# Fused two-block transformer: what fills TensorE beside a recurrent branch, and which engine squares the decays

## The chip, the cores and the metric

The kernel runs on one core of one Trainium2 chip. The metric is the device time of one execution in microseconds: 1811.38 us, the median of three runs (1807.41, 1811.38 and 1813.76). Lower is better. The core's engines are TensorE (PE, with its weight loads PEld), VectorE (DVE), ScalarE (ACT), GpSimd (POOL) and SyncE (SP), which issues most of the DMAs.

## The reference, cut to what matters

Two blocks run one behind the other on 512 tokens of width 1024 (plus 16 meta tokens in the first). The change lies in the second block, ahead of its experts. There one normalised input h is projected to q, k, v, to the input and the gate of a recurrent branch, and to two output gates:

```
q, k, v, lru_x, lru_g, gate_pre = split(h @ w_in)
o = diff_attention(rope(rms_norm(q)), rope(rms_norm(k)), v, lam)      # 8 heads, two 64-wide maps each
xr = depthwise_conv(lru_x)
for each direction:
    r, i = sigmoid(xr @ w_a + b_a), sigmoid(xr @ w_i + b_i)           # 8 diagonal blocks of 128
    log_a = -8 * r * softplus(-lam_param);  a = exp(log_a)
    h_dir = scan(a, sqrt(-expm1(2 * log_a)) * (i * xr))
y_lru = (h_fwd + h_bwd) * gelu(lru_g)
merged = g_attn * (norm(o) @ w_attn_o) + g_lru * (y_lru @ w_lru_o)
```

## The kernel before, in words

Everything is kept feature-major in float32. Each large matrix product is made of three matmuls on high and low halves (`mm3`, lines 151 to 153): the weights are loaded by SP in pieces of 1 MB into one of two raw buffers (line 68), ScalarE rounds 1024 columns to the high half (line 145) and VectorE subtracts for the low half (line 146). One such split feeds 24 matmuls of 512 columns, which is one filling step.

A build-time planner orders the instructions of each engine. It takes them by their place in the program and by when it reckons them ready, and may draw later ones forward where an earlier one is not ready. So the generators below give a place in the program, not a fixed time.

Stages that matter, in the order of the program (`block2`):

- **Recurrent branch.** Four groups of two 128-channel blocks. For each block, xr is split to rH and rL (lines 1023 and 1024), four gates are multiplied, and for each direction ScalarE makes two tanh (lines 1034 and 1035), the decay `a` by Exp (line 1036) and another tanh (line 1037); GpSimd squares the decay into `a2` (line 1039), and VectorE makes (a2 + 1) times that tanh (line 1040). Line 1041 forms the gated input on VectorE. At the group's end ScalarE takes the square roots (line 1047, with a load of its table), VectorE multiplies and scans in both directions (lines 1049 to 1051), and GpSimd adds the two scans into `hs`. Behind each group the program takes filling steps: 5, 5, 4 and 4.
- **The filling there** is the projection of q, k and v for the first four heads, then gelu tiles. `qkv2` takes k, q, v in turn, four steps each, and holds four PSUM banks through the four steps. k and q are emptied by ScalarE (a square), by VectorE (lines 1260 to 1262) and by GpSimd (line 1266), then scaled (line 1279 for k); v is emptied by four ScalarE copies (line 1253). A gelu tile takes one bank and one step; `ev_gelu2` empties it by five VectorE and three ScalarE instructions (lines 1001 to 1008), one of which multiplies by `hs`, and leaves lH and lL.
- **Attention 2, first half.** Heads 0 to 3, four steps a head, with more filling: the gelu tiles that are left, the eight tiles of the recurrent branch's output projection (each needs all eight lH and lL; ScalarE copies them out at line 1061), and q, k, v of heads 4 to 7. Nothing is taken at the first two steps, two items at each further one.
- **Attention 2, second half.** Heads 4 to 7, filled by the tiles of the two output gates.

PSUM has four banks for filling in the recurrent branch and the first half (`ps2`), two for scores, one for transposes, one for values. Most large tensors live in a pool of 30 pair buffers (`big`, two tiles of 528 columns each); a new tile waits until one of them is let go.

```python
gelu = self.fm_steps(wi["lru_g"], KD, 8, xH, xL, C0, ev_gelu2)
fill = chain(self.qkv2(0, wi, xH, xL, inv, epsx, qkv[0]), gelu)
...
nc.gpsimd.tensor_tensor(a2, a[:, dd], a[:, dd], op=ALU.mult)
...
for _ in range(5 if grp < 2 else 4):
    next(fill, None)
```

Of the kernel before, what the change touches and what calls it, by code (L numbers as in the profile page):

```python
# [11 lines left out]
F32 = mybir.dt.float32  # L12
# [4 lines left out]
AF = mybir.ActivationFunctionType  # L17
ALU = mybir.AluOpType
AX = mybir.AxisListType

P = 128
D = 1024
KD = D // P
SEQ = 512
# [110 lines left out]
class Builder:  # L135
# [779 lines left out]
    def block2(self, xH, xL, squares, out):  # L915
        nc, A, tc = self.nc, self.A, self.tc
        V, S, E = nc.vector, nc.scalar, nc.tensor
        with ExitStack() as ctx:
# [6 lines left out]
            wi = {k: Weights(self, A["w2_" + k], 1024, 2)  # L925
                  for k in ("q", "k", "v", "lru_x", "lru_g", "g_attn", "g_lru")}
            vx = sm.tile([P, 4], F32, name="vx")
            inv = sm.tile([P, 4], F32, name="inv2")
            inv_b = med.tile([P, SEQ], F32, name="inv_b2", bufs=1)
            epsx = sm.tile([P, 4], F32, name="epsx2")  # L930
# [3 lines left out]
            sp = sm.tile([P, 16], F32, name="sp")  # L934
# [15 lines left out]
            V.tensor_scalar(t, t, 0.0, 0.5, op0=ALU.max, op1=ALU.mult)  # L950
            V.tensor_tensor(sp, sp, t, op=ALU.add)
            spm = {}
            for f in (-8.0, 8.0):
                spm[f] = sm.tile([P, 16], F32, name=f"sp{int(f) + 16}")
                V.tensor_scalar(spm[f], sp, f, None, op0=ALU.mult)
            hb = {}
            for w in ("a", "i"):
# [51 lines left out]

            qkv = [{}, {}]  # L1010
            gelu = self.fm_steps(wi["lru_g"], KD, 8, xH, xL, C0, ev_gelu2)
            fill = chain(self.qkv2(0, wi, xH, xL, inv, epsx, qkv[0]), gelu)
            wl = Weights(self, A["w2_lru"], 1024, 1)
            for grp in range(4):
                wH, wL = [t.rearrange("p (n m c) -> p n m c", n=2, m=4) for t in wl.get(grp)]
                units = []
                for nn in range(2):
                    n = 2 * grp + nn
                    rH = med.tile([P, SEQ], F32R, name="rH", tag="hl")
                    rL = med.tile([P, SEQ], F32R, name="rL", tag="hl")  # L1020
                    ix = med.tile([P, 2, SEQ], F32, name="ix", tag="pr")
                    a, m2 = self.pair("la", F32, (P, 2, SEQ)), self.pair("lm", F32, (P, 2, SEQ))
                    S.copy(rH, xr[n])
                    V.tensor_tensor(rL, xr[n], rH.bitcast(F32), op=ALU.subtract)
                    for dd in range(2):
                        u = 8 * dd + n
                        if dd == 0:
                            pr, pi = [self.ps_sc.tile([P, SEQ], F32, name="sc") for _ in range(2)]
                        else:
                            pr = self.ps_tr.tile([P, SEQ], F32, name="tr")  # L1030
                            pi = self.ps_pv.tile([P, SEQ], F32, name="pv")
                        self.mm3(pr, wH[:, nn, 2 * dd], wL[:, nn, 2 * dd], rH, rL, True, True)
                        self.mm3(pi, wH[:, nn, 2 * dd + 1], wL[:, nn, 2 * dd + 1], rH, rL, True, True)
                        S.activation(m2[:, dd], pr, AF.Tanh, scale=0.5, bias=hb["a"][:, u:u + 1])
                        S.activation(ix[:, dd], pi, AF.Tanh, scale=0.5, bias=hb["i"][:, u:u + 1])
                        S.activation(a[:, dd], m2[:, dd], AF.Exp, scale=spm[-8.0][:, u:u + 1], bias=spm[-8.0][:, u:u + 1])
                        S.activation(m2[:, dd], m2[:, dd], AF.Tanh, scale=spm[8.0][:, u:u + 1], bias=spm[8.0][:, u:u + 1])
                        a2 = med.tile([P, SEQ], F32, name="a2", tag="pT", bufs=2)
                        nc.gpsimd.tensor_tensor(a2, a[:, dd], a[:, dd], op=ALU.mult)
                        V.scalar_tensor_tensor(m2[:, dd], a2, 1.0, m2[:, dd], op0=ALU.add, op1=ALU.mult)  # L1040
                    V.scalar_tensor_tensor(ix, ix, 1.0, xr[n][:, None, :].to_broadcast([P, 2, SEQ]),
                                           op0=ALU.add, op1=ALU.mult)
                    units.append((n, a, m2, ix))
                zero = sm.tile([P, 1], F32, name="zero", bufs=2)
                V.tensor_scalar(zero, units[-1][2][:, 1, :1], 0.0, None, op0=ALU.mult)
                for n, a, m2, ix in units:
                    S.activation(m2, m2, AF.Sqrt, scale=0.25, bias=zero)
                for n, a, m2, ix in units:
                    V.tensor_tensor(ix, ix, m2, op=ALU.mult)
                    V.tensor_tensor_scan(hs[n], a[:, 0], ix[:, 0], 0.0, op0=ALU.mult, op1=ALU.add)  # L1050
                    V.tensor_tensor_scan(m2[:, 1, ::-1], a[:, 1, ::-1], ix[:, 1, ::-1], 0.0, op0=ALU.mult, op1=ALU.add)
                    nc.gpsimd.tensor_tensor(hs[n], hs[n], m2[:, 1], op=ALU.add)
                for _ in range(5 if grp < 2 else 4):
                    next(fill, None)
# [14 lines left out]
            def ev_gattn(m, ps, c0, n):  # L1069
# [7 lines left out]
            o = {}  # L1077
            fill = chain(gelu,
                         self.fm_steps(Weights(self, A["w_lru_o_2"], 1024, 2), KD, 8, lH, lL, C0, ev_lru_o),
                         self.qkv2(1, wi, xH, xL, inv, epsx, qkv[1]))  # L1080
            for step, _ in enumerate(self.attention2(0, qkv[0], ld, gs, o)):
                for _ in range(2 if step >= 2 else 0):
                    next(fill, None)
            for _ in fill:
                pass
            fill = chain(self.fm_steps(wi["g_lru"], KD, 8, xH, xL, C0, ev_glru),
                         self.fm_steps(wi["g_attn"], KD, 8, xH, xL, C0, ev_gattn))
# [134 lines left out]
            V.tensor_tensor(Sn[:, :, 32:], Sn[:, :, 32:], g[:, None, :32].to_broadcast([P, 4, 32]), op=ALU.mult)  # L1222
            self.TC2[w], self.TS2[w] = C, Sn

    def qkv2(self, b, wi, xH, xL, inv, epsx, out):

        nc = self.nc
        V, S = nc.vector, nc.scalar
        sm, med = self.sm, self.med
        if b == 0:  # L1230
            self.rope2_tables()
        for w in ("k", "q", "v"):
            tl = []
            for j in range(0, 4, 2):
                t = self.pair(w + "t", F32, (P, 2, SEQ))
# [3 lines left out]
            for i in range(4):  # L1239
                wH, wL = [t.rearrange("p (k c) -> p k c", k=2) for t in wi[w].get(4 * b + i)]  # L1240
                for j in range(4):
                    ts = slice(j * P, (j + 1) * P)
                    for kk in range(2):
                        k = 2 * i + kk
# [5 lines left out]
            for j in range(4):  # L1250
                ps = pss[j]
                if w == "v":
# [12 lines left out]
                                op=ALU.mult)  # L1265
# [546 lines left out]
```

## Time and profile before

| what | value |
|---|---|
| median of three runs | 1811.38 us |
| the profiled execution's own time | 1810.2 us |
| its span, first to last instruction | 1808.2 us |
| mean granted TensorE clock | 0.984 |
| TensorE busy | 1740.5 us, 96% |
| VectorE busy | 1215.0 us, 67% |
| ScalarE busy | 925.2 us, 51% |
| GpSimd busy | 264.8 us, 15% |
| recurrent branch, groups 0 to 3 | from 936 us to about 1090 us |
| attention 2, first half | to about 1246 us |

Times in the profile are microseconds from the span's start. Busy shares of the whole span are means over stages that have different limits, so the stages are looked at one by one. In a row of the timeline the bracket at the end is the engine's idle time just before, and what ended it. The granted clock is a mean over a stretch: 1.00 is 2.4 GHz, and at 1.2 GHz it would be 0.50.

### The profile page before, as it was taken

The numbers are of one execution on the slowest core, as the hardware profiler recorded it, in microseconds if no ns is written. First come the engines' busy times: TensorE is split into PE (matmuls) and PEld (weight loads), VectorE is DVE, ScalarE is ACT, GpSimd is POOL, SyncE is SP. The second block draws the span as 40 slices with busy tenths as digits, with TensorE's granted clock in tenths as the row PEclk, the third lists the DMA queues.
The fourth block names the chain that finished last, engine by engine and source line by source line (L and its number), as shares of the span: only waits on it lengthen the run. The fifth ranks groups of instructions, "written<-read, shape, count | busy, mean of one in ns | idle before, by whom it ended". The sixth has DMA issues, their size and how long they took to land. (4 is left out here: it accounts for less than half of the span.)

```text
span 1808.2 us, 25732 instructions
## 1 busy us (share of the span) xinstructions
PE 1740.5 (96%) x9706; PEld 1466.3 (81%) x9706; DVE 1215.0 (67%) x2264; ACT 925.2 (51%) x1545; POOL 264.8 (15%) x249
## 2 busy tenths in 40 slices
PE   7999999999999999999999898999999997999997
PEld 7889899999976878888877676777787886888885
DVE  7475555456457555446599988586776528999996
ACT  5343244433344234433336666545665335888885
POOL 3102300001210320000203321020101031111111
PEclk9999999999999999999999999999999997999999
DMA  4122121224322122223522222222115588999993
GB/s 146 59 89 71 53 69 51 75 77 142 109 77 93 53 70 70 70 82 106 170 90 70 85 90 71 70 70 70 53 65 190 184 282 298 384 383 387 381 383 64
DMA packets 69089, 244.36 MB, mean 135 GB/s; under 512 B 10848, under 2 KB 20064, under 8 KB 57056
## 3 DMA queue, kind: packets, MB, share of 16 engines
q1 hardware_dynamic: 63200, 221.69, 34.3%
q0 software_dynamic: 4608, 16.78, 3.6%
q10 hardware_dynamic: 1152, 4.19, 0.7%
q8 instruction: 78, 1.28, 0.3%
q14 instruction: 51, 0.42, 0.1%
HBM read 225.20 MB, written 17.37 MB: 134 GB/s over the span
## 5 line engine op out<-in xcount | busy, mean ns | idle before, releaser
L145 ACT CAST wh<-raw 128x1024 fp32r<-128x1024 f32 (+2 forms) x206 | 212.0, 1030 | 415.9 <-PE mm L152 335.7
L146 DVE TENSOR_TENSOR wl<-raw,wh 128x1024 fp32r<-128x1024 f32 (+2 forms) x206 | 253.4, 1232 | 103.9 <-ACT wh L145 102.2
L151 PE MATMUL mm<-xH,wh 128*128 128x264 f32 (+1 forms) x912 | 292.3, 321 | 10.8 <-ACT xH L361 8.7
L152 PE MATMUL mm<-xL,wh 128*128 128x264 f32 (+1 forms) x912 | 291.4, 320 | 0.7 <-DVE xL L362 0.5
L153 PE MATMUL mm<-xH,wl 128*128 128x264 f32 (+1 forms) x912 | 290.7, 319 | 0.0
L146 DVE TENSOR_TENSOR wl<-we,wh 128x1024 fp32r<-128x1024 f32 x192 | 227.5, 1222 | 15.7 <-ACT wh L145 13.0
L145 ACT CAST wh<-we 128x1024 fp32r<-128x1024 f32 x192 | 198.4, 1049 | 42.2 <-PE mm L153 32.5
L151 PEld LDWEIGHTS mm<-xH,wh 128*128 128x128 f32 x912 | 174.7, 192 | 24.0 <-ACT xH L361 8.7
L152 PEld LDWEIGHTS mm<-xL,wh 128*128 128x128 f32 x912 | 174.4, 192 | 11.5 <-DVE xL L362 1.4
L153 PEld LDWEIGHTS mm<-xH,wl 128*128 128x128 f32 x912 | 174.6, 192 | 10.4
L151 PE MATMUL mm<-wh,eH 128*128 128x512 f32 x256 | 104.4, 408 | 0.0
L151 PE MATMUL mm<-x2H,wh 128*128 128x512 f32 x256 | 102.1, 399 | 0.0
L152 PE MATMUL mm<-x2L,wh 128*128 128x512 f32 x256 | 101.9, 398 | 0.0
L153 PE MATMUL mm<-x2H,wl 128*128 128x512 f32 x256 | 101.8, 398 | 0.0
L153 PE MATMUL mm<-wh,eL 128*128 128x512 f32 x256 | 101.3, 396 | 0.0
L152 PE MATMUL mm<-wl,eH 128*128 128x512 f32 x256 | 101.0, 394 | 0.0
L126 POOL TENSOR_TENSOR z<-z,sq 128x528 f32<-128x528 f32 (+1 forms) x26 | 43.2, 1664 | 330.3 <-ACT sq L365 256.7
L151 PE MATMUL mm<-wh,x2H 128*128 128x512 f32 x192 | 77.5, 404 | 4.8 <-DVE rt__9342 L1262 2.8
L152 PE MATMUL mm<-wl,x2H 128*128 128x512 f32 x192 | 76.5, 399 | 0.0
L153 PE MATMUL mm<-wh,x2L 128*128 128x512 f32 x192 | 76.5, 402 | 0.0
L789 ACT ACTIVATE pr<-sc,bi,r3q 128x264 f32<-128x264 f32 (+3 forms) x80 | 46.6, 589 | 55.0 <-DVE bi L787 54.3
L151 PE MATMUL mm<-mgH,wh 128*128 128x264 f32 (+1 forms) x192 | 61.7, 321 | 0.0
(621 smaller groups left out, 4052.0 us busy)
## 6 DMA issues: line engine op xcount, KB each, us to landing
we<-in_w_moe SPq DMA_DIRECT2D x184, 512.0 KB
raw<-in_w_out SPq DMA_DIRECT2D x12, 1024.0 KB
raw<-in_w_g_mla SPq DMA_DIRECT2D x8, 1024.0 KB
raw<-in_w_g_pool SPq DMA_DIRECT2D x8, 1024.0 KB
raw<-in_w_c_q SPq DMA_DIRECT2D x6, 1024.0 KB
raw<-in_w_q_b SPq DMA_DIRECT2D x6, 768.0 KB
raw<-in_w_z_mla SPq DMA_DIRECT2D x4, 1024.0 KB
raw<-in_w_u_pool SPq DMA_DIRECT2D x4, 1024.0 KB
```

Of the source, the lines that this page charges most:

```text
L126: self.kb.nc.gpsimd.tensor_tensor(self.sum[:, off:], self.sum[:, off:], sq[:, off:], op=ALU.add)
L145: nc.scalar.copy(H[:, :F], src)
L146: lo.tensor_tensor(L[:, :F], src, H[:, :F].bitcast(F32), op=ALU.subtract)
L151: mm(out, lH, rH, start=start, stop=False)
L152: mm(out, lH, rL, start=False, stop=False)
L153: mm(out, lL, rH, start=False, stop=stop)
L789: S.activation(pr[:, a:b, e], scs[q], AF.Exp, bias=bi[:, e:e + 1], scale=c, accum_out=su[:, e, q:q + 1])
```

## The change

Three edits, all in the second block. First, the filling of the recurrent branch has v of heads 4 to 7 put between q, k, v of heads 0 to 3 and the gelu tiles; 18 steps are taken there as before, so 12 of the first half, 4 of v and 2 gelu tiles. Second, attention 2's first half is then filled by six gelu tiles, the output projection and k, q of heads 4 to 7 (22 items as before), with one item taken at each of the first two steps, where none was. Third, `a2` is made by ScalarE as Exp with twice the factor, from the tanh ahead of the one that overwrites it, and no longer by GpSimd as a product; a third scaled column, spm[-16.0], serves it.

```diff
-            for f in (-8.0, 8.0):
-                spm[f] = sm.tile([P, 16], F32, name=f"sp{int(f) + 16}")
+            for f in (-16.0, -8.0, 8.0):
+                spm[f] = sm.tile([P, 16], F32, name=f"sp{int(f) + 16}_")
                 V.tensor_scalar(spm[f], sp, f, None, op0=ALU.mult)
...
-            fill = chain(self.qkv2(0, wi, xH, xL, inv, epsx, qkv[0]), gelu)
+            fill = chain(self.qkv2(0, wi, xH, xL, inv, epsx, qkv[0]), self.qkv2(1, wi, xH, xL, inv, epsx, qkv[1], "v"), gelu)
...
                         S.activation(a[:, dd], m2[:, dd], AF.Exp, scale=spm[-8.0][:, u:u + 1], bias=spm[-8.0][:, u:u + 1])
+                        a2 = med.tile([P, SEQ], F32, name="a2", tag="pT", bufs=2)
+                        S.activation(a2, m2[:, dd], AF.Exp, scale=spm[-16.0][:, u:u + 1], bias=spm[-16.0][:, u:u + 1])
                         S.activation(m2[:, dd], m2[:, dd], AF.Tanh, scale=spm[8.0][:, u:u + 1], bias=spm[8.0][:, u:u + 1])
-                        a2 = med.tile([P, SEQ], F32, name="a2", tag="pT", bufs=2)
-                        nc.gpsimd.tensor_tensor(a2, a[:, dd], a[:, dd], op=ALU.mult)
...
-                         self.qkv2(1, wi, xH, xL, inv, epsx, qkv[1]))
+                         self.qkv2(1, wi, xH, xL, inv, epsx, qkv[1], "kq"))
             for step, _ in enumerate(self.attention2(0, qkv[0], ld, gs, o)):
-                for _ in range(2 if step >= 2 else 0):
+                for _ in range(2 if step >= 2 else 1):
                     next(fill, None)
...
-    def qkv2(self, b, wi, xH, xL, inv, epsx, out):
+    def qkv2(self, b, wi, xH, xL, inv, epsx, out, names="kqv"):
...
-        for w in ("k", "q", "v"):
+        for w in names:
```

## Rows read from the trace of the kernel before

**Rows 1.** The page, busy time of each engine over the span.
```profile
PE 1740.5 (96%) x9706; PEld 1466.3 (81%) x9706; DVE 1215.0 (67%) x2264; ACT 925.2 (51%) x1545; POOL 264.8 (15%) x249
```

**Rows 2.** Stretches, groups 0 to 3, scans, seam, first half: us busy, PEclk, DMA.
```profile
936.00:966.00 30.00, 28.86 (x126) 23.04 (x125) 24.43 (x25) 21.25 (x28) 7.64 (x5) 1.00 0.19 58
966.00:1000.00 34.00, 29.86 (x121) 23.22 (x120) 32.41 (x48) 24.53 (x32) 11.72 (x10) 0.95 0.26 85
1000.00:1034.00 34.00, 30.68 (x120) 23.95 (x120) 30.09 (x44) 21.56 (x28) 13.70 (x10) 0.90 0.25 84
1034.00:1062.00 28.00, 25.90 (x111) 20.43 (x111) 22.24 (x24) 18.14 (x27) 5.77 (x4) 1.00 0.26 92
1062.00:1090.00 28.00, 28.00 (x124) 22.54 (x122) 26.51 (x30) 18.36 (x24) 7.07 (x4) 1.00 0.25 80
1090.00:1110.00 20.00, 15.83 (x64) 11.82 (x64) 18.90 (x35) 12.87 (x24) 4.31 (x4) 0.91 0.12 48
1110.00:1246.00 136.00, 132.99 (x651) 104.98 (x651) 90.95 (x202) 70.50 (x144) 18.80 (x20) 1.00 0.23 78
```

**Rows 3.** TensorE's timeline, its longest waits between 936 and 1110 us.
```profile
945.29 0.50 PE L152 MATMUL sc<-rL,wh 128*128 128x512 f32 x1 [1.14 <-DVE rL L1024]
...
969.33 0.47 PE L151 MATMUL mm<-wh,x2H 128*128 128x512 f32 x1 [2.77 <-DVE rt__9342 L1262]
...
999.87 0.50 PE L151 MATMUL sc<-rH,wh 128*128 128x512 f32 x1 [1.13 <-ACT wh L145]
...
1003.09 0.73 PE L153 MATMUL sc<-rH,wl 128*128 128x512 f32 x2 [1.32 <-DVE wl L146]
...
1006.52 0.80 PE L151 MATMUL mm<-wh,x2H 128*128 128x512 f32 x1 [2.00 <-DVE rt__9608 L1262]
...
1035.25 0.50 PE L151 MATMUL sc<-rH,wh 128*128 128x512 f32 x1 [1.13 <-ACT wh L145]
...
1059.79 0.50 PE L152 MATMUL sc<-rL,wh 128*128 128x512 f32 x1 [0.97 <-DVE rL L1024]
...
1095.97 0.63 PE L1300 MATMUL tr<-ident,qt 128*128 128x128 f32 x4 [2.80 <-DVE kl L1304]
```

**Rows 4.** Groups of VectorE, 936 to 1110 us: count, busy, mean ns, idle before.
```profile
L146 DVE TENSOR_TENSOR wl<-raw,wh 128x1024 fp32r<-128x1024 f32 x25 | 32.2, 1289 | 8.8 <-ACT wh L145 8.7
...
L1005 DVE SCALAR_TENSOR_TENSOR z<-th,z 128x512 f32<-128x512 f32 x8 | 7.0, 881 | 2.3 <-ACT th L1004 2.3
...
L1001 DVE TENSOR_TENSOR z<-mm,inv_b 128x512 f32<-128x512 f32 x8 | 5.5, 685 | 2.0 <-PE mm L153 2.0
```

**Rows 5.** The squares on GpSimd, and VectorE's lines beside them (last: min/median/max).
```profile
L1039 POOL TENSOR_TENSOR a<-la 128x512 f32<-128x512 f32 x16 | 21.0, 1316 | 91.8 <-ACT la L1036 91.8
...
L1041 DVE SCALAR_TENSOR_TENSOR ix<-ix,xr 128x1024 f32<-128x1024 f32 x8 | 13.2, 1653 | 0.2 <-ACT ix L1035 0.2
...
L1024 DVE TENSOR_TENSOR rL<-xr,rH 128x512 fp32r<-128x512 f32 x7 | 6.4, 914 | 0.0
...
L1279 DVE TENSOR_TENSOR kt<-kt,rk 128x512 f32<-128x512 f32 x4 | 4.2, 1104 | 0.0
...
L1041 DVE SCALAR_TENSOR_TENSOR ix<-ix,xr x8: 1214/1644/2111, 942.6 to 1067.1; 128x1024 f32<-128x1024 f32 x8
```

**Rows 6.** ScalarE's timeline: an Exp and its follower, and group 1's square root.
```profile
951.69 0.81 ACT L1036 ACTIVATE la<-lm,sp 128x512 f32<-128x512 f32 x1
952.40 0.61 ACT L1023 CAST rH<-xr 128x512 fp32r<-128x512 f32 x1
...
993.89 1.15 ACT L1047 ACTIVATE lm<-lm,zero 128x1024 f32<-128x1024 f32 x1 [3.03 <-DVE zero L1045]
```

**Rows 7.** TensorE's timeline, behind the k projection of heads 4 to 7.
```profile
1188.15 0.63 PE L1332 MATMUL tr<-ident,pr 128*128 128x128 f32 x4 [0.20 <-DVE pr L1329]
```

**Rows 8.** ScalarE's timeline, copies of the output projection (fourth and fifth, then two more).
```profile
1135.52 1.07 ACT L1061 COPY gp<-mm 128x512 f32<-128x512 f32 x2
...
1154.08 1.07 ACT L1061 COPY gp<-mm 128x512 f32<-128x512 f32 x2 [0.33 <-PE mm L152]
```

## The prediction, written before the changed kernel ran

> **What bounds the kernel now.** I read the page first: TensorE is busy for 1740.5 us, 96% of the span of 1808.2 us [rows 1], so it can only win where it waits or runs slowly. The page's chain of waits holds nothing but the last GpSimd steps and is no help for the middle, so I went to the stretches. The change touches three stages of the second block: the recurrent branch (four groups of two channel blocks, 936 to about 1090 us), attention 2's first half (to about 1246 us) and the seam between them. A table by stage [rows 2] gives the loss of TensorE, idle time plus lost clock (stretch times one minus the granted clock: at 1.2 instead of 2.4 GHz half of the time is lost):
> - group 0: 30.00 - 28.86 = 1.1 us idle;
> - group 1: 4.1 idle + 0.05 x 34 = 1.7 of clock;
> - group 2: 3.3 idle + 3.4 of clock;
> - group 3: 2.1 idle;
> - the seam, 1090 to 1110: 4.2 idle + 1.8 of clock;
> - the rest of the first half, 136 us long: 3.0 idle.
> Together about 22 us up to 1110 us and 3 after it. That is all a change of the filling can win here: TensorE's own work is the same before and after, matmul for matmul, and only moves. VectorE is busy for 32.4 of 34 us in group 1, 30.1 of 34 in group 2, 26.5 of 28 from 1062 on and 18.9 of 20 in the seam, but for only 91 of 136 us after it [rows 2]. Then TensorE's own timeline names what ended each wait [rows 3]: rL at 945 and 1060 (VectorE's low half of the gates' input), the rotated k and q at 969 and 1006 (VectorE empties PSUM late, behind the scans), the weight split at 1000, 1003 and 1035, and at 1096 attention's low half kl. Twelve waits make the 14.9 us; the eight longest are shown (the longest left out is 0.79, for the last gelu tiles' lH at 1091). VectorE in the recurrent branch is the limit that shows through.
>
> **The change, part by part.** Durations are of the profiled execution, 1810.2 us (1808.2 of span and 2.0 around it). The median of the three runs is 1811.4, so 1.2 above it.
>
> *1. Values in place of gelu tiles, recurrent branch.* The 18 filling steps were 12 of qkv(0) and 6 gelu; they become 12, 4 of the second half's v, and 2 gelu. A step of either is 24 matmuls, so TensorE's cover is equal, and each takes one split of 1024 weight columns. What differs is the emptying: a gelu tile costs VectorE five instructions, 30.6 us for eight tiles over five lines (5.5 to 7.0 a line, the shortest and the longest shown [rows 4]), 3.8 us a tile; the v stage has four ScalarE copies in all. So four tiles, 15 us of VectorE, leave groups 2 and 3. That removes the rL wait of group 3 (0.97, behind gelu work): -1.0. The weight-split waits at 1000 and 1035 (1.13 each) stand at the head of a group and wait for TensorE to release a weight buffer; the same number of splits passes, so they stay. The two extra v weight loads on SP replace two lru_g loads of the same size there: nothing; their cover is the same 5.6 us of matmuls a step.
>
> *2. Six gelu tiles, not two, in attention 2's first half.* Before, gelu 6 and 7 and then the output projection (which needs all eight lH and lL) come straight behind the scans, and the last tiles are emptied by a VectorE that is still late: the seam's 4.2 + 1.8 = 6.0 us. After, TensorE has six gelu tiles (six times 24 matmuls at 0.23 us, 33 us) before it needs any of them, held only by four PSUM banks. VectorE's load there is then six tiles x (3.8 + 1.3 for the split [rows 4]) = 31 us beside 33 of TensorE plus one head of attention, so it is nearly full, but without the scans ahead of it. At best the seam costs nothing more (-6.0); at worst the same projection waits as long for the same eighth tile (0). I take -4.5, nearer to the first, since VectorE has 45 us free in the 136 after the seam [rows 2].
>
> *3. The squared decays on ScalarE.* Sixteen GpSimd products of 1.3 us [rows 5] go. GpSimd slows VectorE when both run: the 1024-wide product of line 1041 takes 1.21 us alone and up to 2.11, 13.2 us for eight where 9.7 would do; likewise rL 6.4 for seven where 7 x 0.68 = 4.8 would do, and k's scaling 4.2 where 4 x 0.68 = 2.7 would do [rows 5]; the gelu product of line 1005 takes 7.0 where 5.5 would do [rows 4]. That is 3.5 + 1.6 + 1.5 + 1.5 = 8 us of VectorE, which I take to come back over four groups. The Trainium skill, page "SBUF — State Buffer", section "Who interferes with whom", says that VectorE and GpSimd share one port pair by an exclusive lock, so that the later one blocks for the other's whole instruction when VectorE reads two SBUF inputs; by that rule alone up to 16 x 1.3 = 21 us would come back (an estimate), the trace shows under half of it, and the seam and groups would win some 3 us more. ScalarE pays: an exponential of this size holds it for 0.71 us from start to start [rows 6], 16 x 0.71 = 11.4 us, 2.8 a group, where ScalarE is two thirds busy [rows 2]. In group 1 it stands still for 3.03 us waiting for VectorE ahead of the square roots [rows 6]; there the 2.8 is hidden and the roots, which start when VectorE is through, come about 2 us earlier. With them the q emptying: of the waits of 1.32 and 2.00 at 1003 and 1006 I take 2.0 off and, of group 2's 3.4 us of lost clock that follows them, 1.7: -3.7 (bounds 0 and -6.7). In group 0 ScalarE runs without a break from 946 to the roots (two of its starts, 0.71 apart, in [rows 6]), so two extra exponentials of the second unit move roots, scans and k emptying by 1.4 us, and the wait of 2.77 at 969 grows by that, while the rL wait at 945 shrinks by 0.5: +0.9. Bounds for group 0: -1.1, if its rL wait goes and nothing follows, and +2.8. In group 2 ScalarE is as dense ahead of the roots and the v copies: +0.5 (bounds 0 and +1.4). GpSimd's other products (hs, k, q) only come earlier. The third scaled column (16 wide, once) is under 0.2 us: nothing, beside the convolution.
>
> *4. The end of the first half.* k and q of the second half now close the filling where v did: 22 items before and after, but one starts at each of the first two steps, so the last head has none of its own. q's four banks need VectorE (about 2 us each) before gate tiles can use them, where v needed four ScalarE copies. The nearest row is the same hand-over at the end of the second half's k, where TensorE waits 0.20 [rows 7]; the far one is 2.77 plus clock in group 1 [rows 3]. I take +1.0, the near row plus some, with bounds 0 and +4.5.
>
> *5. Memory.* Two more pair buffers are held through the first half (v, two pairs), and the pool of 30 is full there already: the projection's copies stop at 1135.5 with five made and go on at 1154 [rows 8], when a head's keys are let go: 8 pairs of input, 6 of q, k, v, 8 of lH and lL, 5 copies and 3 of heads make 30. After, three copies fit and PSUM holds four more tiles: seven of eight. I take 0, with up to +10 below.
>
> Sum: -1.0 - 4.5 - 3.7 + 0.9 + 0.5 + 1.0 = -6.8 us; 1810.2 - 6.8 = 1803.4 for a run like the profiled one, and 1804.5 with the 1.2 of the median.
>
> **The rivals.**
> A. *The losses only change places.* VectorE's work is the same but for the 8 us, the seam's projection still waits for the eighth gelu tile, and each group still ends in roots, scans, emptying. For it: waits of group 0 to 2 (8.6 of 14.9) lie where the filling does not change. Against it: VectorE's 45 free us later on. Parts 1 and 2 give 1.5, part 3 nothing: 1810.
> B. *Slower: the pool of 30 pair buffers decides.* Place: the output projection, while v of the second half lies in two of them. It decides once the fourth copy must wait for a head to end with PSUM's four banks full. Then TensorE has only one head's rows; the standstill of the copies was 18.6 us (1135.5 to 1154.1) under cover of other matmuls; if half of that is uncovered and drops the clock as in the seam (1.8 for 4.2 idle), it is 9.3 + 4.0 = 13 us on top of -6.8: 1818. Against it: heads have precedence and the first keys go in time.
> C. *ScalarE becomes the chain of every group*: 2.8 us later roots four times, 11.2, against the 5.5 of parts 1 and 2, and 1.2 for the median: 1817. Against it: its 3.03 us of standing still in group 1, and that it is only two thirds busy.
> D. *More*: the seam and VectorE's contention both go fully, clock included: -1.0 - 6.0 - 6.7 = -13.7, so 1798. For it: the clock falls only after waits, so that one shorter wait can save twice.
>
> **How the numbers follow.** Forecast 0.50, its own range 1800 to 1809; A 0.20; B 0.09; C 0.09; D 0.12. About 0.3%, 5.4 us, is what a measurement of this kernel tells from no change: faster is below 1806. Of the forecast 0.42 lies there and 0.08 within; with D 0.54 faster; with A 0.28 the same; B and C 0.18 slower. The range of 8 in 10 reaches from near D to the lower part of B and C: 1797 to 1814.
>
> **What would show it.** Right: no rL wait in group 3; under 2 us of idle at the seam and full clock in it; line 1041 near 1.2 us throughout; ScalarE some 11 us busier between 936 and 1110; the roots of group 1 earlier against its gates. Wrong: waits at 969 and 1006 as long or longer with the clock at half behind them; TensorE idle in the output projection or in the last head; copies of the projection waiting for buffers over more than one head. If the stretch from 936 to 1246 loses 25 us again, A was right.

## The result and the profile after

The changed kernel takes 1825.76 us (median of 4 runs, 1824.25 to 1826.35) against 1810.18 (4 runs): a ratio of 1.0084, interval 1.0071 to 1.0098. It is 15.6 us slower; 6.8 faster was forecast, and the range ended at 1814. The profiled execution took 1826.2 us, with a span of 1823.9. The page, as in [rows 1]:

```profile
PE 1745.1 (96%) x9706; PEld 1471.0 (81%) x9706; DVE 1207.2 (66%) x2265; ACT 937.0 (51%) x1561; POOL 244.9 (13%) x233
```

VectorE has 7.8 us less, where 8 was forecast; ScalarE 11.8 more (11.4); GpSimd 20 less. Engine by engine the change costs and saves what it was taken to, so the loss is one of order. The stretches of the changed kernel, with those of [rows 2] and two more:

```profile
936.00:966.00 30.00, 30.00 (x131) 24.20 (x130) 21.96 (x26) 23.95 (x33) 0.84 (x1) 1.00 0.23 77
966.00:1000.00 34.00, 29.68 (x121) 23.39 (x120) 30.51 (x48) 27.38 (x36) 8.72 (x6) 0.95 0.26 88
1000.00:1034.00 34.00, 30.04 (x120) 23.18 (x120) 28.16 (x44) 23.34 (x31) 9.56 (x6) 0.95 0.19 64
1034.00:1062.00 28.00, 26.87 (x116) 21.54 (x116) 18.08 (x17) 22.59 (x31) 3.42 (x2) 1.00 0.28 96
1062.00:1090.00 28.00, 23.23 (x98) 18.45 (x97) 22.03 (x25) 17.89 (x24) 6.42 (x6) 0.94 0.20 71
1090.00:1110.00 20.00, 19.75 (x98) 15.60 (x98) 18.36 (x38) 12.97 (x29) 0.00 (x0) 1.00 0.30 106
1110.00:1246.00 136.00, 130.04 (x625) 102.76 (x623) 91.08 (x189) 68.49 (x136) 14.08 (x15) 1.00 0.20 70
1246.00:1280.00 34.00, 28.61 (x142) 23.11 (x143) 25.07 (x66) 16.51 (x40) 4.33 (x5) 0.85 0.09 32
1380.00:1450.00 70.00, 65.90 (x301) 51.88 (x300) 44.49 (x90) 31.13 (x58) 4.87 (x14) 0.98 0.48 175
```

The last two stretches in the kernel before:

```profile
1246.00:1280.00 34.00, 33.58 (x174) 26.40 (x173) 25.88 (x64) 21.60 (x49) 2.44 (x4) 1.00 0.18 63
1380.00:1450.00 70.00, 69.83 (x330) 57.08 (x329) 38.08 (x70) 26.51 (x46) 4.51 (x12) 1.00 0.65 235
```

TensorE's loss, counted as in the prediction (idle plus stretch times one minus the granted clock), goes from 13.7 to 11.7 us in groups 0 to 2 (936 to 1034), from 8.1 to 7.8 in group 3, branch's end and seam (1034 to 1110), from 3.4 to 16.4 in 1110 to 1280, and from 0.2 to 5.5 in 1380 to 1450. That is -2.0 - 0.3 + 13.0 + 5.3 = +16.0 us; the span grew by 15.7. From 1450 us on everything is merely later.

This counting, the prediction's too, charges a low clock twice where TensorE stands still while the clock is low. The largest case is here (changed kernel):

```profile
1246.00:1251.00 5.00, 0.02 (x1) 0.05 (x1) 4.83 (x10) 0.58 (x1) 3.80 (x5) 0.50 0.00 0
1251.00:1256.30 5.30, 5.30 (x15) 4.34 (x16) 3.42 (x11) 1.16 (x2) 0.53 (x1) 0.50 0.00 0
```

Of the 5.1 us of lost clock in 1246 to 1280 only the second row's 2.6 (half of 5.3) are lost work; the others lie in idle time that is counted already. So 1110 to 1280 costs 10.5 us, not 13.0, and the stages make +13.5. Of the rest, the branch's first gate matmul accounts for 1.4: it already starts that much later (937.97 against 936.55), ahead of the stages in question; why is open. The waits behind these numbers, from TensorE's timeline (compare [rows 3]):

```profile
971.92 0.47 PE L151 MATMUL mm<-wh,x2H 128*128 128x512 f32 x1 [3.19 <-DVE rt__9344 L1262]
...
1007.65 0.79 PE L151 MATMUL mm<-wh,x2H 128*128 128x512 f32 x1 [2.45 <-DVE rt__9610 L1262]
...
1068.59 0.79 PE L151 MATMUL mm<-x2H,wh 128*128 128x512 f32 x1 [4.77 <-ACT vt L1253]
...
1250.98 1.09 PE L1300 MATMUL tr<-ident,qt 128*128 128x128 f32 x4 [9.49 <-DVE kl L1304]
1251.72 0.78 PE L152 MATMUL mm<-x2L,wh 128*128 128x512 f32 x1
...
1391.16 0.50 PE L1322 MATMUL sc<-kh,q 128*128 128x512 f32 x1 [1.78 <-ACT pr L1326]
```

The rL waits and the wait at the seam are gone, as forecast. New are 4.77 us at the branch's end, 9.49 in the first half's last head, and the end of the second half.

**The hole of 9.49 us.** VectorE's timeline of the changed kernel, with the emptying of q (L1260 to L1262), its normalization (L1271) and head 3's key halves (L1304):

```profile
1240.91 1.81 DVE L146 TENSOR_TENSOR wl<-raw,wh 128x1024 fp32r<-128x1024 f32 x1
...
1246.23 0.67 DVE L1262 TENSOR_TENSOR rt__11573<-mm,TS2q 128x512 f32<-128x512 f32 x1
1246.83 0.50 DVE L1271 SCALAR_TENSOR_TENSOR ssq<-ssq,epsx 128x32 f32<-128x32 f32 x1
1247.25 0.67 DVE L1304 TENSOR_TENSOR kl<-tr,kh 64x512 fp32r<-64x512 f32 x1
...
1250.14 0.69 DVE L1304 TENSOR_TENSOR kl<-tr,kh 64x512 fp32r<-64x512 f32 x1
```

The key transposes were done at 1239.8. Their halves stand in VectorE's queue behind the rest of q's emptying; until the second one has read the only transposes bank, the query transposes can't start, and they are next on TensorE. The gate tile's matmul at 1251.72 stands behind them, though its weights and its data had been there since its neighbours of 1241. From 1251.7 to 1256 matmuls follow each other at 0.43 us instead of 0.23: some 2.6 us more, about 12 in all. In the kernel before, VectorE made the same halves when q was long empty, and TensorE had v's matmuls up to 1242:

```profile
1235.12 0.67 DVE L1304 TENSOR_TENSOR kl<-tr,kh 64x512 fp32r<-64x512 f32 x1
...
1237.86 0.69 DVE L1304 TENSOR_TENSOR kl<-tr,kh 64x512 fp32r<-64x512 f32 x1
```

**The 4.77 us at the branch's end.** ScalarE's timeline of the changed kernel:

```profile
1063.42 1.04 ACT L145 CAST wh<-raw 128x1024 fp32r<-128x1024 f32 x1 [0.36 <-PE mm L153]
1064.48 1.28 ACT L1047 ACT_TABLE_LOAD   x1
1065.78 2.19 ACT L1047 ACTIVATE lm<-lm,zero 128x1024 f32<-128x1024 f32 x2
1067.87 2.40 ACT L1253 ACTIVATE vt<-mm,inv 128x512 f32<-128x512 f32 x4
```

v was ready in PSUM at 1063; its copies come after a cast, a table load and the roots, and the next gelu tile waits for one of its four banks.

**Where the filling lies.** Filling matmuls (L151 to L153) between one head's key transposes and the next, counted in the timelines; for head 7 without the output's projection behind it:

| kernel | head 0 | 1 | 2 | 3 | 4 | 5 | 6 | 7 |
|---|---|---|---|---|---|---|---|---|
| before | 125 | 163 | 192 | 86 | 82 | 89 | 94 | 81 |
| changed | 192 | 192 | 192 | 53 | 87 | 96 | 93 | 55 |
| before, 1 at the first two steps | 144 | 192 | 192 | 62 | 82 | 89 | 94 | 57 |
| changed, 0 at the first two steps | 145 | 191 | 203 | 70 | 87 | 89 | 94 | 81 |
| before, 28 pair buffers | 125 | 163 | 192 | 64 | 95 | 273 | 0 | 0 |

With one item at each of the first two steps the 22 items run out with head 2. Heads 3 to 6 then use 26 gate matmuls more than before (53 - 38 in head 3, where 48 of the 86 are v's, and 11 in heads 4 to 6), and the second half's last head has 26 fewer: that is the loss at 1391.

### The profile page after: what moved, and what is told of

Its sections match the earlier page's. It is cut to its first block, busy times and chain, and to the rows that moved or that the text cites. A ratio compares the mean times of both kernels' runs of the same rounds, so it can differ in the third digit from the quotient of the medians.

```text
span 1823.9 us, 25710 instructions
## 1 busy us (share of the span) xinstructions
PE 1745.1 (96%) x9706; PEld 1471.0 (81%) x9706; DVE 1207.2 (66%) x2265; ACT 937.0 (51%) x1561; POOL 244.9 (13%) x233
## 4 chain that ended last, share of the span: by engine, by line
PE 88%; DVE 7%; ACT 2%; DMA 1%; issue 1%; POOL 0%; SPq 0%; POOLq 0%; ACTq 0%; DVEq 0%
PE mm L151 24%; PE mm L152 24%; PE mm L153 24%; PE pv L819 2%; DVE wl L146 2%; PE sc L781 2%; PE pv L1336 2%; PE tr L806 1%; PE sc L1322 1%; ACT wh L145 1%; PE tr L1332 1%; PE tr L1557 1%; PE sc L1323 1%; PE sc L554 1%; PE pv L813 1%
## 5 line engine op out<-in xcount | busy, mean ns | idle before, releaser
L151 PE MATMUL mm<-xH,wh 128*128 128x264 f32 (+1 forms) x912 | 292.3, 321 | 11.0 <-ACT xH L361 8.9
L153 PE MATMUL mm<-xH,wl 128*128 128x264 f32 (+1 forms) x912 | 291.1, 320 | 0.0
L151 PEld LDWEIGHTS mm<-xH,wh 128*128 128x128 f32 x912 | 174.7, 192 | 24.1 <-ACT xH L361 8.9
L153 PEld LDWEIGHTS mm<-xH,wl 128*128 128x128 f32 x912 | 174.8, 192 | 10.3
L151 PE MATMUL mm<-x2H,wh 128*128 128x512 f32 x256 | 103.9, 406 | 5.3 <-ACT vt L1253 4.8
L151 PE MATMUL mm<-wh,eH 128*128 128x512 f32 x256 | 104.6, 409 | 0.0
L153 PE MATMUL mm<-x2H,wl 128*128 128x512 f32 x256 | 103.3, 404 | 0.0
L153 PE MATMUL mm<-wh,eL 128*128 128x512 f32 x256 | 101.4, 396 | 0.0
L151 PE MATMUL mm<-wh,x2H 128*128 128x512 f32 x192 | 76.8, 403 | 5.6 <-DVE rt__9344 L1262 3.2
L153 PE MATMUL mm<-wh,x2L 128*128 128x512 f32 x192 | 76.8, 403 | 0.0
L1326 ACT ACTIVATE pr<-sc,bi,rq 128x512 f32<-128x512 f32 x64 | 49.5, 778 | 26.1 <-DVE bi L1325 26.0
```

What stands on the lines that cost most here:

```text
L151: mm(out, lH, rH, start=start, stop=False)
L153: mm(out, lL, rH, start=False, stop=stop)
L1326: S.activation(pr[:, c], sc, AF.Exp, bias=bi[:, c1], scale=cc[:, c1], accum_out=su[:, c1])
```

## The experiments

Theory 1 is the hole's: q closes the filling, and its emptying by VectorE keeps the last head's keys waiting, with a bare end of the second half in its train. The rivals to begin with: the squares on ScalarE (S), and the two pair buffers of v that are held longer (M). Ratios are to the kernel before in the same session (1809.3 to 1810.4 us); the wait rows are of TensorE's timeline.

**1. The squares alone** (before, with the change's Exp in place of the GpSimd product).

> Only the squares move to ScalarE; the filling is that of the kernel before. Main theory (the 15.6 us come from the last head of attention 2's first half, where VectorE empties q of heads 4 to 7 ahead of the head's own key halves and TensorE stands 9.5 us, 12 with the slow clock behind it): none of that here, so within 4 us of before, 1807 to 1814. Rival S (ScalarE's 16 extra exponentials, 0.71 us each, delay roots and copies): most of the loss is here, 1819 to 1826. Rival M (two of the 30 pair buffers held longer): as the main theory, within 4 us.

1814.17 us, ratio 1.0026 (1.0013 to 1.0038), just above the main theory's range. The hole isn't there. The squares alone are slower, by a wait at head 0's end, where head 0's own chain finds no filling because the projection's copies are late:

```profile
1129.87 0.63 PE L1346 MATMUL pv<-ident,ot 128*128 128x128 f32 x4 [3.53 <-DVE ot L1344]
1131.81 0.80 PE L151 MATMUL mm<-lH,wh 128*128 128x512 f32 x1 [1.31 <-ACT gp L1061]
```

**2. The filling alone** (the change, with the squares on GpSimd).

> Only the filling changes; the squares stay on GpSimd. Main theory: the wait for the key halves of the first half's last head is there again, 8 to 11 us, and the time is 1820 to 1828. Rival S: at most 1814, and the wait behind the value copies at the branch's end (4.8 us) is gone. Rival M: 1820 to 1828 too, but with idle time in the output projection.

1828.32 us, 1.0108 (1.0092 to 1.0123), just above the main theory's range, with waits of 4.77 and 9.48 us in the same places. So S falls: the filling makes the loss, and beside it the squares on ScalarE give some 4 us back by the ratios (1.0108 against 1.0084), with an uncertainty nearly as large.

**3. The first two steps empty again.**
```diff
-                for _ in range(2 if step >= 2 else 1):
+                for _ in range(2 if step >= 2 else 0):
```


> The change, but no filling item at attention's first two steps, as before, so that the filling ends one step later, inside the last head, and q's last two steps stand behind the last head's key halves in the program. Main theory: VectorE splits the keys first, the wait falls from 9.5 to under 3 us and the slow clock behind it goes: 1811 to 1817. Rival M: the buffers are held as long as in the change, so 1823 to 1828. Rival S: 1823 to 1828.

1818.95 us, 1.0055 (1.0041 to 1.0069), above the main theory's range. The single hole breaks up into waits of 1.24, 1.87, 1.88, 1.59 and 0.68 us at half clock, and the end of the second half is whole (81 matmuls, TensorE busy for 69.83 of 70 us). The first half's end is hardly better; the changed kernel and this one, from 1110 to 1280:

```profile
1110.00:1280.00 170.00, 158.65 (x767) 125.87 (x766) 116.14 (x254) 85.01 (x176) 18.42 (x20) 0.97 0.18 62
...
1110.00:1280.00 170.00, 160.93 (x770) 127.17 (x769) 116.50 (x258) 87.38 (x179) 20.37 (x21) 0.96 0.20 69
```

(The x behind TensorE's time counts its matmuls; the kernel before has 823.) So of the 6.8 us that came back, some 5.3 are the second half's. The step at which the filling ends is a part of the loss, but it does not by itself close the hole.

**4. Key halves with precedence** (the change, `high_priority` around the copies and differences of L1302 and L1304).

> The change, with the planner's precedence given to the halves of keys and queries (ScalarE copy, VectorE subtraction); nothing else. VectorE now has the first key half behind four of q's eight products instead of all eight, the second behind six. Main theory: the wait shrinks with the products taken out from ahead of it, from 9.5 to 4 to 7 us, and the time to 1818 to 1823. Rivals S and M: no change, 1823 to 1828.

1821.17 us, 1.0075 (1.0062 to 1.0089). The hole shrinks to 7.33 us: two of q's four tiles and a weight split of 1.79 us still come ahead of the first half.

**5. v's copies with precedence too.**

> The change with precedence for the key and query halves (as in the run before) and for the four value copies. If the copies' place behind the square roots makes the 4.8 us wait at the branch's end, it falls to under 1.5 us and the slow clock behind it goes: 1813 to 1817 against 1821. If the wait is for the last value matmuls or for the roots themselves, it stays and so does the time, 1820 to 1823.

1823.86 us, 1.0081 (1.0065 to 1.0096), and the 4.77 us stay: the copies still follow the roots.

**6. The kernel before with 28 pair buffers instead of 30.**

> The kernel before with 28 pair buffers in place of 30, so that the projection has as few as in the change; no other edit. Rival M (the buffers decide): at least 6 us slower, 1816 to 1826, with TensorE idle in the projection or the heads beside it. Main theory: PSUM's banks and the other heads cover it, within 4 us of before.

1859.47 us, 1.0273 (1.0257 to 1.0289). By stages most of it, 25.8 us of added idle and up to 11.9 of clock (in part counted twice), lies behind 1380:

```profile
1380.00:1450.00 70.00, 44.03 (x217) 30.91 (x216) 37.62 (x117) 34.26 (x92) 6.84 (x18) 0.83 0.15 58
```

Head 5 runs through 273 matmuls of gates, and heads 6 and 7 have none. The pool is at its limit in the second half, where the change holds no more than before. In the first half, where it does, two buffers fewer cost the kernel before about 7 us (1110 to 1280), so M was possible there. It falls with runs 7 and 13, which hold as many buffers as the change and lose the hole. In the changed kernel itself the projection's copies stop at three for some 20 us (1149.22 to 1169.44), and TensorE is busy for 119.24 us of 1110 to 1230.

**7. k instead of v in the branch**, so that q and v close the filling.
```diff
-self.qkv2(1, wi, xH, xL, inv, epsx, qkv[1], "v"), gelu)
+self.qkv2(1, wi, xH, xL, inv, epsx, qkv[1], "k"), gelu)
...
-self.qkv2(1, wi, xH, xL, inv, epsx, qkv[1], "kq"))
+self.qkv2(1, wi, xH, xL, inv, epsx, qkv[1], "qv"))
```


> The change with k of heads 4 to 7, not v, in the recurrent branch; q and then v close the first half's filling, as before. The buffers held are as many and the gelu tiles lie as in the change. Main theory (the stage that closes the filling decides, since v's banks come free by ScalarE copies and q's only behind VectorE): the wait of 9.5 us in the last head goes, to under 2 us, and the loss with it; k's emptying in group 3 costs 3 to 5 us in place of the 4.8 of the v copies: 1806 to 1813. Rival M and a rival by which any filling stage that ends a step earlier leaves the last head bare: 1819 to 1826.

1824.17 us, 1.0075 (1.0061 to 1.0088): the time was missed. At the place that theory 1 speaks of it held, with all of q's emptying still on VectorE and the filling still ending with head 2: the last head's wait is 2.03 us, and from 1110 to 1280 TensorE loses 5.3 us where the changed kernel loses 16.4 (counted as in the prediction):

```profile
1110.00:1280.00 170.00, 166.45 (x817) 132.49 (x816) 110.55 (x242) 94.36 (x196) 13.33 (x16) 0.99 0.20 69
```

But k's emptying stands behind the last scans, and the branch's end lost more than the last head won (clock 0.76 from 1062 to 1090):

```profile
1077.85 0.77 PE L151 MATMUL mm<-x2H,wh 128*128 128x512 f32 x1 [12.82 <-DVE rt__10094 L1262]
```

**8. The kernel before with 2 instead of 4 items in the branch's last two groups.**

> The kernel before, squares on GpSimd, with 5, 5, 2 and 2 filling steps in the branch: four gelu tiles go to the first half, v stays last, nothing else moves. If the gelu tiles in the branch made the seam's loss and v last keeps the last head covered: the seam's 4.2 us of idle falls to under 2 and the time to 1802 to 1808. If the planner draws the gelu tiles into the branch anyway: 1808 to 1812. If the branch lacks cover: slower, 1813 to 1820, with new waits in groups 2 and 3.

1813.42 us, 1.0016 (1.0007 to 1.0025). The wait for kl at the seam becomes 3.96 us: moving VectorE's gelu work out of the branch does not by itself mend the seam. The branch also lacks cover, as the third guess had it: TensorE waits 1.97 us for rL at 1047.6.

**9. The kernel before with one item at each of the first two steps.**

> The kernel before with one edit: one filling item instead of none at each of attention 2's first two steps, so that the 22 items run out one step earlier, with head 2, and the last head of the first half has none of its own; v, which four copies on ScalarE empty, still closes them, and the squares stay on GpSimd. Theory 1 (the last head lost its cover because q, which VectorE empties, closes the filling and holds the four banks that the gate tiles need): no wait over 2 us in the last head's own stretch, 1806 to 1815 us. Rival (running out one step earlier is enough to leave the last head bare): 5 us or more of idle in it, its matmuls at half clock, 1818 to 1825.

1817.28 us, 1.0041 (1.0027 to 1.0054), between the two. Ending one step early costs about 7.5 us even where v closes: k's emptying now runs into the start of head 2 (1.47 us for kl, then 0.48), head 3 waits 2.22 for its own, and the second half's last head has 57 matmuls and loses 3 us.

**10. Gate tiles from the second half's second step on** (the change, `if step >= 1`).

> The changed kernel, with the second half's gate tiles drawn from its second step on instead of the first. Theory 1 (the loss of 5.3 us in the last head of the second half comes from gate tiles that were spent early, in the hole at the end of the first half, so that the last head has 55 matmuls of filling in place of 81): the last head has 75 or more, its four waits of 0.5 to 1.8 us go, and the end of the first half stays as it is or is up to 3 us worse: 1819 to 1824 us. Rival (the second half's end is late for a reason of its own, or the gates would be missed more at the start): 1825 to 1831, with the waits still there or an equal loss in head 4.

1823.45 us, 1.0081 (1.0067 to 1.0095): the time lies in theory 1's range, but its means failed. The last head still has 55 matmuls, so where a gate tile is drawn did not move it. That the planner places it by what it finds ready is likely and not shown.

**11. v's copies on VectorE, with precedence.**

> The changed kernel, but the four values of the second half are scaled out of PSUM by VectorE, with precedence, instead of ScalarE. Theory 1 (the new wait of 4.77 us at the end of the recurrent branch is the v copies' place on ScalarE, behind the last gates' exponentials, a weight cast, the table load and the roots): the wait falls under 1 us and the clock stays at full there, 1817 to 1821 us. Rival (VectorE is no earlier, because these copies come behind its scans, as the emptying of k did): wait of 5 to 13 us, 1826 to 1835.

1828.62 us, 1.0105 (1.009 to 1.0121). The rival was right:

```profile
1068.21 0.80 PE L151 MATMUL mm<-x2H,wh 128*128 128x512 f32 x1 [7.33 <-DVE vt L1254]
```

**12. Two items for six steps, then one.**
```diff
-                for _ in range(2 if step >= 2 else 1):
+                for _ in range(2 if step < 6 else 1):
```


> The changed kernel with its 22 filling items drawn two a step for the first six steps of attention 2's first half and then one a step to its end, so that k and q last until the last head. Theory 1 (a head's step needs about one item beside it, and the end of the first half is lost because the last head has none): no wait over 2 us within the last head; some of it comes back at the hand-over, where the next head's queries are needed as soon as they are made, 2 to 8 us: 1812 to 1821. Rival (the loss stands wherever q is emptied, for VectorE is then late for the head beside it): 10 us or more of idle and lost clock in the last head or at the hand-over, 1823 to 1830.

1834.02 us, 1.0136 (1.0121 to 1.0152), above even the rival's range. The rival's mechanism again: at one item a step the emptying of k and of q each leave holes of their own, at the end of heads 2 and 3 and at the hand-over to the second half:

```profile
1222.25 0.63 PE L1346 MATMUL pv<-ident,ot 128*128 128x128 f32 x4 [4.26 <-DVE rs_y L170]
...
1265.26 1.09 PE L1346 MATMUL pv<-ident,ot 128*128 128x128 f32 x4 [4.62 <-DVE rs_y L170]
...
1276.44 1.09 PE L1300 MATMUL tr<-ident,qt 128*128 128x128 f32 x4 [6.54 <-DVE kl L1304]
```

**13. q emptied by ScalarE.**
```diff
-                if w == "v":
+                if w == "v" or (w == "q" and b == 1):
                     S.activation(tl[j], ps, AF.Copy, scale=inv[:, j:j + 1])
                     continue
```


> The changed kernel with the second half's q emptied as v is: four scaled copies on ScalarE. It leaves out q's rotation and its normalization for heads 4 to 7 (their softmax scale is a constant), and with them twelve VectorE instructions of 0.7 us, four GpSimd sums, four squares on ScalarE and the square root's iteration. Theory 1 (VectorE's emptying of q, and not the mere lack of items, leaves the last head bare): the wait of 9.5 us ahead of the last head's query transposes falls under 2 us and the clock stays up, 1810 to 1816 us. Rival (the filling ran out one step early, and that decides): 5 us or more of waits in that head remain, 1820 to 1826.

1815.58 us (9 runs), 1.0028 (1.0018 to 1.0038): 10 us come back, with the order of the change untouched. But the work is gone too and not only moved: VectorE is busy for 10.7 us less (1207.2 to 1196.5). The hole of 9.49 becomes

```profile
1247.05 0.63 PE L1306 MATMUL tr<-ident,qt 128*128 128x128 f32 x4 [2.21 <-DVE kl L1310]
```

From 1110 to 1280 TensorE loses 5.3 us, as in 7, where no work is left out. With both, theory 1 stands for this place, if not under the 2 us that it had guessed. Of the 5 us still missing, 3 are the end of the second half (57 matmuls), where TensorE is busy for 67.04 of 70 us.

**14. The change, and 15. the kernel before, filled from the fourth step on** (`2 if step >= 3 else 0`).

> The changed kernel, with its filling drawn from the fourth step of attention 2's first half on, two a step, so that it ends two steps later than in the change, inside the last head. Theory 2 (half of the loss is the step at which the filling ends: each step later gave 6.8 us back): the last head has 90 or more filling matmuls and no wait over 2 us, and the first head, with nothing beside it but its own work, gives 1 to 4 us of that away: 1811 to 1818 us. Theory 1 alone (q must be emptied by VectorE beside some head in any case, and that head waits): 8 us or more lost there, 1818 to 1823.

> The kernel before, with its filling drawn from attention 2's fourth step on instead of the third, so that v closes it one step later. Theory 2: the last head is covered already in the kernel before, nothing is left to win there, and the first head loses up to 3 us: 1808 to 1814 us. Rival (later is better still, as one step earlier was 7.8 us worse): 1803 to 1807.

The change: 1817.41 us, 1.0048 (1.0034 to 1.0061), inside theory 2's range, but not by its means: a wait of 3.70 us for an exponential is left in the last head, 1110 to 1280 still loses 11.5 us against 3.4 in the kernel before, and most of the gain is the second half, where TensorE is busy for 69.86 of 70 us. The kernel before: 1824.18, 1.0079 (1.0065 to 1.0093), missed: its first head has 102 filling matmuls instead of 125 and pays for the later end with

```profile
1123.63 1.06 PE L1346 MATMUL pv<-ident,ot 128*128 128x128 f32 x4 [3.65 <-DVE ot L1344]
```

and 8.1 us of idle from 1110 to 1180. Its start at the third step is the best of the three tried: a step earlier costs 7.5 us, a step later 14.

**16. The kernel before with the key halves first** (as in 4).

> The kernel before, with precedence for the copies and the differences that make each head's high and low halves of keys and queries. If the wait for kl of 2.80 us at the seam with the half clock behind it is only their place in VectorE's queue: it falls under 1 us, 1804 to 1808 us. Rival (what is put off in their place, the last gelu tiles or the running head's maxima, is waited for instead): 1809 to 1815.

1814.89 us, 1.0022 (1.0012 to 1.0032), in the rival's range. Precedence doesn't shorten the wait at the seam (3.15 us).

**17. v drawn a group earlier, and 18. the same with the filling from the fourth step on.**
```diff
-                for _ in range(5 if grp < 2 else 4):
+                for _ in range((5, 5, 6, 2)[grp]):
```


> The changed kernel with the four groups of the recurrent branch drawing 5, 5, 6 and 2 filling items in place of 5, 5, 4 and 4: the second half's v is then wholly drawn in the third group, so that its copies stand on ScalarE ahead of the last group's exponentials, table load and roots; everything from attention 2 on stays. Theory 1 (the 4.77 us at the branch's end is the v copies' place behind the last roots): the wait goes, with the half clock behind it, and the last head of the first half keeps its 9.5 us: 1818 to 1822 us. Rival (the last group, with two items in place of four, then waits for its own gates and roots as long): 1824 to 1829.

> The same 5, 5, 6 and 2 items, and the filling of attention 2's first half drawn from its fourth step on, as in the run that ended it inside the last head. If the losses are separate places, their cures add up: 1817.4 of that run less the 4 to 7 us of the branch's end, 1810 to 1814 us, about the kernel before. Below 1806 only if the seam's win shows in full. Rival (VectorE's work comes late again in the first head, which now starts with nothing beside it): 1816 to 1822.

1828.32 us, 1.0103 (1.0088 to 1.0119), and 1823.93, 1.0073 (1.0059 to 1.0086): both theories missed; 17 lies in its rival's range, though not for the rival's reason, and 18 above its rival's. v's copies now come ahead of the last group's ScalarE work and the 4.77 us go, but a shorter wait for them stands a group earlier, and with only gelu tiles taken behind the last group the wait of the seam is back (the rows are of 17; 18 has both, too):

```profile
1038.51 0.50 PE L151 MATMUL mm<-wh,x2H 128*128 128x512 f32 x1 [2.76 <-ACT vt L1253]
...
1104.33 0.89 PE L1300 MATMUL tr<-ident,qt 128*128 128x128 f32 x4 [3.96 <-DVE kl L1304]
```

None of the versions tried is faster than the kernel before.

## Why the prediction was wrong, point by point

**Part 4 failed**, "the end of the first half": +1.0 with bounds 0 and +4.5 was the term for k and q closing the filling, and 13.0 us was measured there in the prediction's counting, 10.5 without what that counts twice. The text saw that the last head has no item of its own and that q's banks need VectorE, and it named idle time in the last head as a sign of being wrong. But it priced only the hand-over of the banks, from the row of 0.20 [rows 7], which stands where two items a step still lie beside. It left out who stands behind q's emptying on VectorE: the last head's own key halves, which hold the transposes bank and with it TensorE's next instruction. With q's emptying off VectorE (13), or with v and not q closing the filling (7), the loss of this stretch falls from 16.4 to 5.3 us. What is left above the 3.4 of the kernel before goes with the step at which the filling ends: one step early cost that kernel 3.3 us there (6.7 against 3.4) and some 3 in the second half, 7.5 in all (9). One step later gave the changed kernel 6.8 back, nearly all of it in the second half (3).

**Left out altogether:** the second half, +5.3 us. It was taken to be untouched, but the planned order spends 26 more gate matmuls in heads 3 to 6 and leaves so many fewer for the last head. In each kernel whose filling ended with head 2 and not later (changed, 2, 4, 5, 7, 9 to 11, 13 and 17) TensorE loses 3 to 6 us there (3 in 7, 9 and 13); in those that ended later, 0 to 2, the one with 28 buffers aside. That the first half's draws decide it is shown, by 3 against the change and 9 against the kernel before, each one edit; why the planner orders the gates so is not.

**Parts 1 and 2** (-1.0 and -4.5): the mechanism held and the gain did not. The rL wait of group 3 is gone, the seam's loss fell from 6.0 to 0.25 us. But "the v stage has four ScalarE copies in all" was counted as work and not by its place behind the last roots: 4.77 idle plus 0.06 x 28 = 1.7 of clock came back at the branch's end. Net -0.3. With v done a group earlier the seam pays (17), with v's last steps in the last group its copies do, with k there the branch's end waits 12.8 us (7); none of these orders was free.

**Part 3** (-3.7 + 0.9 + 0.5 = -2.3): -2.0 was measured in groups 0 to 2, and between the change with and without it -4 (2, by the ratios 1.0108 and 1.0084, with about 4 of uncertainty). Alone they made the kernel before 4.7 us slower (1), so the term's sign depends on the order beside it. GpSimd's hold on VectorE is gone as sized; VectorE's groups in the changed kernel, 936 to 1110 us (compare [rows 5]):

```profile
L1041 DVE SCALAR_TENSOR_TENSOR ix<-ix,xr 128x1024 f32<-128x1024 f32 x8 | 9.8, 1220 | 0.0
...
L1024 DVE TENSOR_TENSOR rL<-xr,rH 128x512 fp32r<-128x512 f32 x7 | 4.8, 686 | 2.0 <-ACT rH L1023 2.0
```

9.7 and 4.8 were forecast. The Trainium skill, page "SBUF — State Buffer", section "Who interferes with whom", would by its exclusive lock have let up to 21 us come back (an estimate); VectorE's whole saving is 7.8, so the measured stretch decides, as weighed before. The parts of the term were not right, though. Group 0 won 1.1 us instead of losing 0.9. In group 2 the waits at 1003 and 1006 (1.32 + 2.00) became 0.54, 0.97 and 2.45, longer together: only the clock there (0.90 to 0.95) gave something. Group 1's roots were to come about 2 us earlier; the first came 1.7 us later (995.58 against 993.89), as ScalarE's last tanh of the gates ahead of it was 2.6 us later (988.60 against 986.01). So VectorE's free time shows little on TensorE: its products ahead of the scans wait 1.24 us for these roots at 996.8, and q's emptying comes behind the scans. The prediction's clock term for group 2 also counted some 0.8 us twice, as its half clock began within the wait.

**Part 5** (0): right. TensorE loses under 1 us from 1110 to 1230, the projection included.

**The rivals.** None of the four times came. A comes nearest for the branch and the seam, where losses mostly changed places: 2.3 us were won and not 7.8. By its own sign it was even right, as 936 to 1246 loses 25.5 us in that counting against 24.7; but 4.5 of the 25.5 are the start of the hole, which the sign's stretch cuts in two. A and D needed part 4 to be small; B's place is covered (6); C's later roots show in group 1, but its chain of four did not form. The one on the slower side was sought in memory and in ScalarE, the two resources that the change visibly adds to, and not in the order of the queue whose load it lightens.

## What to carry to other kernels

Where a stage of an in-order filling is moved, ask of each emptying not how long it is but which instructions of the stage beside it stand behind it on that engine, and what TensorE has next when they are late. Close a filling with the stage whose emptying is on the engine that the next stage needs least, and try the step at which it ends: in the kernel before, one step earlier and one later were both slower. A gain at one seam is sure only when the last item at the neighbouring seams has been looked at too.

## What was not expected of the hardware

A wait costs more than its length, but here not in proportion to it. Behind the 9.49 us TensorE worked at half clock (1.2 GHz) for some 5.3 us, which is 2.6 us on top. Behind the 4.77 us it was 3.4 us, which is 1.7 on top:

```profile
1068.50:1071.90 3.40, 3.31 (x8) 2.64 (x9) 3.40 (x4) 1.77 (x4) 0.11 (x1) 0.50 0.00 0
```

The stretch with the wait of 1.13 us at 1035 has the full clock. The clock was already at half for the last 5 us of the long wait, so a stretch's mean clock (0.85 over 1246 to 1280) says more than was lost. And 28 buffers instead of 30 cost 49 us, more than half of it as idle time 250 us behind the place where the pool was first taken to be full [rows 8].
